# Block-product chunks of a feed-forward layer: the place of two down slabs and of one product, and the homes of the raw blocks

## The chip, the cores and the metric

The kernel runs on one core of a Trainium2 chip. The metric is the device time of one launch in microseconds, as the median of several runs. One more run is recorded by the hardware profiler, and all durations of single instructions come from that execution. The engines are TensorE (PE in the profile, with PEld for its weight loads), VectorE (DVE), ScalarE (ACT), GpSimd (POOL) and SyncE (SP), which here only issues DMA transfers. Each engine works through a queue of its own in order; semaphores tie the queues together.

## The reference

The kernel computes two layers of a model on 256 tokens of width 1024, all in float32. A layer has four stages, each closed by a layer norm over the residual sum. Two of the four are feed-forward stages (FFN), and only those are touched here:

```python
def swiglu(x, w_gate, w_up, w_down):
    return (jax.nn.silu(x @ w_gate) * (x @ w_up)) @ w_down

for l in range(DEPTH):
    h = layer_norm(ALPHA * h + 0.5 * swiglu(h, ffn1_gate[l], ffn1_up[l], ffn1_down[l]), ...)
    ...   # mixer, cross attention
    h = layer_norm(ALPHA * h + 0.5 * swiglu(h, ffn2_gate[l], ffn2_up[l], ffn2_down[l]), ...)
```

`w_gate` and `w_up` are 1024 x 2816, `w_down` is 2816 x 1024.

## The kernel before, in words

**Precision.** TensorE multiplies in a reduced float32 form, so each float32 operand is split in two parts (`split`, L60-62): ScalarE casts the high part (`whi`, L61) and VectorE subtracts it from the source to get the low part (`wlo`, L62). A product is then three matmuls: high by high, low by high, high by low (`product`, L109-112). Each weight tile that arrives by DMA (128 x 1024 float32, 512 KB, called `raw`) costs one cast and one subtraction. High and low parts go round over eight buffers each; raw tiles with the tag `raw` go round over six.

**An FFN.** `ffn` (L407) cuts the 2816 inner columns in six chunks, five of 512 and one of 256, and writes the work of a chunk after the other (main loop, L727-755). Chunk 0 is made by `first`, chunk 5 by `last_hidden`, and the others by `hidden` or, where the chunk's number is in `sevens` (L694), by `by_seven` (L575-667). `sevens` is (2, 3, 4), except for the first FFN of layer 0, where it is (3, 4): eleven chunks in all. When the activations of a chunk exist, `turn` (L451-464) deals them out with four DMA issues on SP (L455), transposes them on VectorE (L458) and splits them. They are then multiplied with the rows of `w_down`: `slab(c, u)` (L688) loads half `u` of chunk `c`'s rows (two raw tiles, so two casts and two subtractions) and `both(c, u)` (L711-717) issues its 24 matmuls for all four output quarters (eight products of three). These add over all chunks into four banks of PSUM with the tag `dn`; the chunks' own products use four banks with the tag `acc`.

**A chunk of block products.** Gate and up chunk are each cut in two by rows: `w00` (gate, rows 0-3 of eight row tiles), `w10` (gate, rows 4-7), `w01` (up, 0-3), `w11` (up, 4-7). Each block is two raw tiles. With tokens in two halves as well, a plain evaluation takes eight products of 12 matmuls; `by_seven` takes seven, with sums of blocks on the weights' side (additions on VectorE, L606, in place in the raw tiles) and sums of quarters of x on the other side (`bx`, made once for an FFN). The products, in the order of the code before:

1. `w00` into bank `o[0]`
2. `w00 + w01` into `o[1]`
3. `w00 + w01 + w11`, added to what is in `o[0]`
4. `w10` into `o[2]`
5. `w01 + w11`, added to `o[0]`
6. `w11`, added to `o[1]`
7. `w00` with gate's rows 4-7 added to it (after the third product the raw tile is reduced and refilled so by an accumulating DMA that GpSimd issues, L644), added to `o[0]`

Since several products add to one bank, what the bank holds in between has to be copied out before the next may add to it: `taken` (L634-635) is a ScalarE copy of `o[0]`, done after products 1, 3 and 5. `put` (L624-625) is a VectorE addition or subtraction of a bank and a stored half. `left` closes the chunk (activation, last subtraction, the product gate by up at L664, and `turn`).

**Homes.** The raw tiles of the blocks live in borrowed places: a pair `spare0`, `spare1`, a pair `lng`, `lnb` (free until the layer norm's parameters are loaded into them by `ln_params`, L300-305, after the last block chunk), and tiles of the tag `raw`. In the kernel before, `w00` and `w01` exchange the first two pairs from chunk to chunk, `w11` is always in two `raw` tiles, and `w10` in `spare2` and a `raw` tile (L595-600).

**The order of the work.** The order in which the code issues instructions is not quite the order in which they run: a scheduler, when the kernel is built, sorts the instructions of each engine into one fixed queue by the dependencies and its own estimates. At run time each queue is served in order. A DMA issue stands in the queue of SP (or GpSimd) and waits there until its target is free.

The three FFNs with three block chunks have the same order on all engines, in either kernel.

Of the kernel before, what the change touches and what calls it, by code (L numbers as in the profile page):

```python
# [11 lines left out]
AF = mybir.ActivationFunctionType  # L12
ALU = mybir.AluOpType
# [4 lines left out]
P = 128  # L18
# [10 lines left out]
CHUNK = 512  # L29
# [17 lines left out]
def model(ctx: ExitStack, tc: tile.TileContext, t: dict, out: bass.AP):  # L47
    nc = tc.nc
# [5 lines left out]
    def acc(shape=(P, 2, SEQ), tag="acc"):  # L54
        return ps.tile(list(shape), F32, tag=tag, name=tag)
# [4 lines left out]
    def split(hi, lo, src):  # L60
        nc.scalar.copy(hi, src)  # L61
        lows.append(nc.vector.tensor_tensor(lo, src, hi.bitcast(F32), op=ALU.subtract))  # L62
# [73 lines left out]
    def mm_rows(o, xh, xl, wh, wl, start, stop, more=False):  # L136
        product(o, xh, wh, start, False, more)
        product(o, xh, wl, False, False, more)
        product(o, xl, wh, False, stop, more)

    def tok(i):
        return slice(i * P, (i + 1) * P)
# [264 lines left out]
    def ffn(l, name, n, pend=None, last=False, early=None):  # L407
        gate, up, down = (t[f"{name}_{x}"][l] for x in ("gate", "up", "down"))
        with tc.tile_pool(name="ffn", bufs=2, reuse_waits="tile") as fp:
# [24 lines left out]
            def ordered(v):  # L434
                return v.rearrange("p (a k j) -> p a k j", a=4, j=32)

            def in_order(o):
                return o.rearrange("p (a j k) -> p a k j", a=4, j=32)
# [136 lines left out]
            def by_seven(c0, bx, between):  # L575
                def rows_by_columns(r):
                    return r.rearrange("p (k c) -> p k c", c=CHUNK)

                def pieces(*tags):
                    return [  # L580
                        rows_by_columns(
                            (fp if "spare" in g else wp).tile([P, DM], F32, tag=g, name="raw", bufs=6 if g == "raw" else 1)
                        )
                        for g in tags
                    ]

                def block(m, j, to):
                    for i in range(2):
                        k = 4 * j + 2 * i
                        loads.append(nc.sync.dma_start(  # L590
                            to[i], m[k * P : (k + 2) * P, c0 : c0 + CHUNK].rearrange("(k p) c -> p k c", p=P)
                        ))
                    return to

                homes = [("spare0", "spare1"), ("lng", "lnb")]  # L595
                turn_of = sevens.index(c0 // CHUNK) % 2
                w00 = block(gate, 0, pieces(*homes[turn_of]))
                w01 = block(up, 0, pieces(*homes[1 - turn_of]))
                w11 = block(up, 1, pieces("raw", "raw"))
                w10 = block(gate, 1, pieces("spare2", "raw"))  # L600

                def parts_of(r, plus=None):
                    hi, lo = [], []
                    for i in range(2):
                        if plus is not None:
                            nc.vector.tensor_tensor(r[i], r[i], plus[i], op=ALU.add)  # L606
                        h = wp.tile([P, 1024], F32R, tag="whi", name="whi", bufs=8)
                        w = wp.tile([P, 1024], F32R, tag="wlo", name="wlo", bufs=8)
                        h, w = (rows_by_columns(x) for x in (h, w))
                        split(h, w, r[i])  # L610
                        hi.append(h)
                        lo.append(w)
                    return Weights(hi, lo, 2, [])

                def part_of_x(i, j):
                    d = slice(4 * j, 4 * j + 4)
                    return xTh[:, d, tok(i)], xTl[:, d, tok(i)]

                def run(o, x, w, more=False):
                    for k in range(4):  # L620
                        wh, wl = w.at(k, slice(0, CHUNK))
                        mm_rows(o, x[0][:, k, :], x[1][:, k, :], wh, wl, k == 0 and not more, k == 3, more)

                def put(o, a, op, b):  # L624
                    nc.vector.tensor_tensor(ordered(o), in_order(a), ordered(b), op=op)

                s = activations()  # L630
                ef = fp.tile([P, NT, CHUNK], F32, tag="up", name="halves", bufs=1)
                e, f = ef[:, 0, :], ef[:, 1, :]

                def taken(o, bank):  # L634
                    nc.scalar.copy(ordered(o), in_order(bank))  # L635

                o = [acc((P, CHUNK)) for _ in range(2)]
                run(o[0], part_of_x(0, 0), parts_of(w00))
                taken(s[:, 0, :], o[0])
                run(o[1], bx[0], parts_of(w00, w01))  # L640
                run(o[0], bx[1], parts_of(w00, w11), True)
                for i in range(2):
                    k = 4 + 2 * i
                    nc.gpsimd.dma_start(  # L644
                        w00[i], gate[k * P : (k + 2) * P, c0 : c0 + CHUNK].rearrange("(k p) c -> p k c", p=P),
                        accum_op=ALU.add,
                    )
                taken(e, o[0])
                o.append(acc((P, CHUNK)))
                run(o[2], part_of_x(0, 1), parts_of(w10))  # L650
                run(o[0], bx[2], parts_of(w01, w11), True)
                put(s[:, 0, :], o[2], ALU.add, s[:, 0, :])
                nc.scalar.activation(s[:, 0, :], s[:, 0, :], AF.Silu)
                taken(f, o[0])
                between()
                put(f, o[1], ALU.subtract, f)
                run(o[1], bx[3], parts_of(w11), True)
                run(o[0], part_of_x(1, 1), parts_of(w00), True)


                def left():
                    activate(s, 1, o[0])
                    put(e, o[1], ALU.subtract, e)
                    nc.vector.tensor_tensor(s, s, ef, op=ALU.mult)  # L664
                    return turn(s)

                return left
# [20 lines left out]
            def slab(c, u):  # L688
                w = load(down, c * 4 + 2 * u, 2, 0, DM, dealt=c < len(chunks) - 1)
                ah, al = acts[c]  # L690
                return w, ah[:, 2 * u : 2 * u + 2, :], al[:, 2 * u : 2 * u + 2, :]


            sevens = (2, 3, 4) if early is None else (3, 4)  # L694
            bx = []
# [7 lines left out]
            chunks = [(c, min(CHUNK, DFF - c)) for c in range(0, DFF, CHUNK)]  # L703
# [7 lines left out]
            def both(c, u):  # L711
                a = slab(c, u)
                for i in range(NT):
                    for k in range(2):
                        for m in range(2):
                            apart = last and i == m == k == u == 1 and c == 3
                            rows_of(a, i, k, m, c == u == k == 0, apart)
# [9 lines left out]
            for c, (c0, ncol) in enumerate(chunks):  # L727
                if not c:
                    acts.append(first())
                    ys = [[acc((P, 512), "dn") for _ in range(2)] for _ in range(NT)]  # L730
                elif c in sevens:
                    left = by_seven(c0, bx, lambda: both(c - 2, 1))
                else:
                    if c in (1, 2) and early is not None:
                        acts.append(hidden(c0, aside))
                    else:
                        acts.append(hidden(c0) if ncol == CHUNK else last_hidden(c0))
                if c == 1 and early is None:
                    bx.extend(blocks_of_x())
                if c == max(sevens) + 1:  # L740
                    gb = ln_params(l, n)
                if c == 1 and early is not None:

                    with tc.issue_after(loads[-1].ins):
                        rest = early(fp)
                if c == 2 and early is not None:
                    with tc.issue_after(lows[-1].ins):
                        rest[0]()
                if c > 0:
                    if c > 1 and c not in sevens:  # L750
                        both(c - 2, 1)
                    if c < len(chunks) - 1:
                        both(c - 1, 0)
                    if c in sevens:
                        acts.append(left())
            end = [slab(4, 0), slab(4, 1), slab(5, 0)]

            def tail(i, m, cols, alone, between):
# [477 lines left out]
```

## Time and profile before

| | |
|---|---|
| median of three runs | 1084.16 us (1083.94 to 1084.78) |
| the profiled execution | 1086.89 us |
| its span (first to last instruction) | 1085.2 us |
| granted TensorE clock, mean | 0.997 |
| TensorE busy | 1059.0 us |
| VectorE busy | 969.0 us |
| ScalarE busy | 669.1 us |
| GpSimd busy | 91.5 us |
| read from device memory | 227.69 MB |

The profile's page gives these totals. The trace behind it can be asked for stretches of time (busy time of each engine, granted clock, DMA share and rate), for an engine's timeline (start and duration of each instruction or group of like ones, and in brackets how long the engine idled before it and what ended the wait), for landing times of DMA transfers, and for the chain of work that ended last. In the rows, L61 and the like are lines of the kernel before; `out<-in` are the program's names. The durations of consecutive instructions on VectorE and ScalarE overlap a little, since the tail of one runs beside the start of the next. Matmuls are pipelined in the same way.

The four stretches with block chunks lie at 76 to 151, 421 to 513, 592 to 685 and 955 to 1047 us.

### The profile page before, as it was taken

What the parts mean: (1) busy time and instruction counts of PE and PEld (TensorE: products, weight loads), DVE (VectorE), ACT (ScalarE), POOL (GpSimd) and SP (SyncE); (2) the same over time, 40 slices, a digit from 0 to 9 for tenths busy, and PEclk for the clock granted to TensorE, in tenths of its full rate; (3) what the DMA queues carried; (4) which work ended last, traced back from release to release, by engine and by line L of the source; (5) the groups of instructions that cost most, each with busy time, mean ns of one, the idle gap of its engine ahead of it and who ended that gap; (6) DMA issues with size and microseconds to landing.
All of it is one profiled execution on the core that took longest, in us unless ns stands there. A gap on an engine that the chain in (4) does not pass through costs nothing.

```text
span 1085.2 us, 16259 instructions
## 1 busy us (share of the span) xinstructions
PE 1059.0 (98%) x5918; PEld 927.8 (85%) x5918; DVE 969.0 (89%) x1279; ACT 669.1 (62%) x920; POOL 91.5 (8%) x136
## 2 busy tenths in 40 slices
PE   9998999999999999999999999999999999999997
PEld 7887788989899888888888887888898998888786
DVE  6979987998998799999899999888989788999996
ACT  7547675767457566567575677666764655667661
POOL 9600001000000000000000000010000000000000
PEclk9999999999999999999999999999999999999999
DMA  9997595755575587679776787957536664786691
GB/s 361 266 290 209 160 322 181 254 195 166 165 271 176 177 278 201 209 259 268 237 276 191 270 271 190 300 181 241 182 131 210 240 238 166 252 271 192 196 291 40
DMA packets 136882, 243.45 MB, mean 224 GB/s; under 512 B 9761, under 2 KB 48961, under 8 KB 136801
## 3 DMA queue, kind: packets, MB, share of 16 engines
q1 hardware_dynamic: 129024, 228.49, 62.4%
q0 software_dynamic: 7200, 12.73, 7.0%
q10 hardware_dynamic: 576, 1.18, 0.3%
q8 instruction: 46, 0.75, 0.3%
q14 instruction: 36, 0.29, 0.1%
HBM read 227.69 MB, written 1.05 MB: 211 GB/s over the span
## 4 chain that ended last, share of the span: by engine, by line
PE 69%; DVE 15%; DMA 7%; issue 5%; ACT 3%; SPq 0%; DVEq 0%; ACTq 0%
PE acc L112 45%; PE dn L112 21%; DVE wlo L62 8%; DMA raw<-in_ffn_up_dram 3%; DMA raw<-in_ffn_gate_dram 3%; DVE raw L606 3%; ACT whi L61 2%; DMA dealt<-sg 1%; PE acc L179 1%; DVE square L458 1%; DVE sg L664 1%; PE dn L938 1%; DVE al L62 1%; DVE sg L445 0%; SPq L455 0%
## 5 line engine op out<-in xcount | busy, mean ns | idle before, releaser
L61 ACT CAST whi<-raw 128x1024 fp32r<-128x1024 f32 (+1 forms) x462 | 463.7, 1041 | 184.4 <-DVE raw L606 79.0
L62 DVE TENSOR_TENSOR wlo<-raw,whi 128x1024 fp32r<-128x1024 f32 (+1 forms) x462 | 542.5, 1207 | 27.2 <-ACT whi L61 24.4
L112 PE MATMUL acc<-whi,xT 128*128 128x512 f32 x872 | 268.5, 381 | 5.0 <-ACT whi L61 4.8
L112 PEld LDWEIGHTS acc<-whi,xT 128*128 128x128 f32 x872 | 164.9, 189 | 30.5 <-ACT whi L61 7.4
L112 PE MATMUL acc<-wlo,xT 128*128 128x512 f32 x436 | 165.8, 380 | 3.5 <-DVE wlo L62 3.5
L112 PE MATMUL acc<-xT,whi 128*128 128x512 f32 x576 | 142.2, 382 | 0.2
L112 PE MATMUL dn<-whi,ah 128*128 128x512 f32 x346 | 130.1, 381 | 1.4 <-ACT whi L61 1.4
L112 PE MATMUL dn<-wlo,ah 128*128 128x512 f32 x346 | 131.4, 380 | 0.0
L112 PE MATMUL dn<-whi,al 128*128 128x512 f32 x346 | 131.1, 379 | 0.0
L112 PEld LDWEIGHTS acc<-xT,whi 128*128 128x128 f32 x576 | 104.0, 190 | 12.5 <-ACT whi L61 0.7
L112 PEld LDWEIGHTS acc<-wlo,xT 128*128 128x128 f32 x436 | 82.4, 189 | 16.8 <-DVE wlo L62 5.4
L112 PE MATMUL dn<-whi,xT 128*128 128x512 f32 x288 | 87.8, 381 | 0.0
L606 DVE TENSOR_TENSOR raw<-raw 128x1024 f32<-128x1024 f32 x66 | 78.7, 1215 | 1.7 <-DMA raw<-in_ffn_up_dram 1.6
L112 PEld LDWEIGHTS acc<-xT,wlo 128*128 128x128 f32 x576 | 75.5, 191 | 3.9
L112 PE MATMUL acc<-xT,wlo 128*128 128x256 f32 x576 | 75.9, 275 | 0.0
L112 PEld LDWEIGHTS dn<-whi,ah 128*128 128x128 f32 x346 | 65.1, 189 | 12.0 <-ACT whi L61 3.0
L112 PE MATMUL acc<-whi,kTh 128*128 128x512 f32 x176 | 68.5, 389 | 5.8 <-ACT sg L635 3.8
L112 PEld LDWEIGHTS dn<-wlo,ah 128*128 128x128 f32 x346 | 65.4, 189 | 10.0 <-DVE wlo L62 0.9
L112 PEld LDWEIGHTS dn<-whi,al 128*128 128x128 f32 x346 | 65.4, 189 | 9.2
L112 PE MATMUL acc<-wlo,kTh 128*128 128x512 f32 x176 | 67.7, 385 | 0.8 <-DVE wlo L62 0.8
L112 PE MATMUL acc<-whi,kTl 128*128 128x512 f32 x176 | 67.5, 383 | 0.0
L112 PEld LDWEIGHTS dn<-whi,xT 128*128 128x128 f32 x288 | 54.4, 189 | 7.7 <-DVE xT L62 0.3
(235 smaller groups left out, 1297.0 us busy)
## 6 DMA issues: line engine op xcount, KB each, us to landing
raw<-in_ffn_up_dram SPq DMA_DIRECT2D x88, 512.0 KB, 5.8
raw<-in_ffn_down_dram SPq DMA_DIRECT2D x88, 512.0 KB, 5.7
raw<-in_ffn_gate_dram SPq DMA_DIRECT2D x84, 512.0 KB, 5.3
raw<-in_w_in_dram SPq DMA_DIRECT2D x48, 512.0 KB, 4.7
raw<-in_ffn_gate_dram POOLq DMA_DIRECT2D x22, 512.0 KB, 6.4
dealt<-sg SPq DMA_DIRECT2D x80, 128.0 KB, 3.2
raw<-in_ca_k_dram SPq DMA_DIRECT2D x16, 512.0 KB, 4.9
raw<-in_w_out_dram SPq DMA_DIRECT2D x16, 512.0 KB, 4.4
```

What stands on the lines that cost most here:

```text
L61: nc.scalar.copy(hi, src)
L62: lows.append(nc.vector.tensor_tensor(lo, src, hi.bitcast(F32), op=ALU.subtract))
L112: nc.tensor.matmul(o, w, x, start=start, stop=stop, skip_group_check=more)
L179: nc.tensor.transpose(pt[:, k, :], src[:, (4 * j + k) * P : (4 * j + k + 1) * P], unit)
L458: nc.vector.transpose(d[:, i].rearrange("p k (b r) -> p b k r", b=4), x[:, :, i, :].rearrange("p b (k j) -> p b k j", k=4),)
L606: nc.vector.tensor_tensor(r[i], r[i], plus[i], op=ALU.add)
L664: nc.vector.tensor_tensor(s, s, ef, op=ALU.mult)
L938: nc.tensor.matmul(o[g, hh, :], kc[:, hh, g], x, start=True, stop=True)
```

## The change

The diff touches `by_seven` and the main loop:

- Three homes instead of two: block chunk number `n` of an FFN puts `w00`, `w01` and `w11` into the homes `n`, `n + 1` and `n + 2` modulo 3, where the third home is two `raw` tiles. `w10` stays in `spare2` and a `raw` tile, and its loads are issued before those of `w11`.
- The product with `w10` (number 4 above) is issued as the third, and its bank is allocated at the start with the two others.
- Half 1 of the down slab of the chunk two before (`both(c - 2, 1)`) is issued ahead of the fifth product instead of between the fifth and the sixth.
- Half 0 of the down slab of the chunk before (`both(c - 1, 0)`), which followed the seventh product, is issued between the fifth product and the sixth.
- `left`, which closes the chunk, follows the seventh product directly.

```diff
-                homes = [("spare0", "spare1"), ("lng", "lnb")]
-                turn_of = sevens.index(c0 // CHUNK) % 2
-                w00 = block(gate, 0, pieces(*homes[turn_of]))
-                w01 = block(up, 0, pieces(*homes[1 - turn_of]))
-                w11 = block(up, 1, pieces("raw", "raw"))
+                homes = [("spare0", "spare1"), ("lng", "lnb"), ("raw", "raw")]
+                n = sevens.index(c0 // CHUNK)
+                w00 = block(gate, 0, pieces(*homes[n % 3]))
+                w01 = block(up, 0, pieces(*homes[(n + 1) % 3]))
                 w10 = block(gate, 1, pieces("spare2", "raw"))
+                w11 = block(up, 1, pieces(*homes[(n + 2) % 3]))
...
-                o = [acc((P, CHUNK)) for _ in range(2)]
+                o = [acc((P, CHUNK)) for _ in range(3)]
                 run(o[0], part_of_x(0, 0), parts_of(w00))
                 taken(s[:, 0, :], o[0])
                 run(o[1], bx[0], parts_of(w00, w01))
+                run(o[2], part_of_x(0, 1), parts_of(w10))
                 run(o[0], bx[1], parts_of(w00, w11), True)
...
+                put(s[:, 0, :], o[2], ALU.add, s[:, 0, :])
                 taken(e, o[0])
-                o.append(acc((P, CHUNK)))
-                run(o[2], part_of_x(0, 1), parts_of(w10))
+                between[0]()
+                nc.scalar.activation(s[:, 0, :], s[:, 0, :], AF.Silu)
                 run(o[0], bx[2], parts_of(w01, w11), True)
-                put(s[:, 0, :], o[2], ALU.add, s[:, 0, :])
-                nc.scalar.activation(s[:, 0, :], s[:, 0, :], AF.Silu)
                 taken(f, o[0])
-                between()
+                between[1]()
                 put(f, o[1], ALU.subtract, f)
                 run(o[1], bx[3], parts_of(w11), True)
                 run(o[0], part_of_x(1, 1), parts_of(w00), True)
...
-                    left = by_seven(c0, bx, lambda: both(c - 2, 1))
+                    left = by_seven(c0, bx, [lambda: both(c - 2, 1), lambda: both(c - 1, 0)])
...
                 if c > 0:
-                    if c > 1 and c not in sevens:
-                        both(c - 2, 1)
-                    if c < len(chunks) - 1:
-                        both(c - 1, 0)
                     if c in sevens:
                         acts.append(left())
+                    else:
+                        if c > 1:
+                            both(c - 2, 1)
+                        if c < len(chunks) - 1:
+                            both(c - 1, 0)
```

## The prediction

> **What bounds the kernel now.** I read the totals by engine first, then busy time by stretch, then VectorE's timeline through one block-product stretch, and last TensorE's gaps and the chain of waits there.
>
> ```profile
> span 1085.2 us, 16259 instructions
> ...
> PE 1059.0 (98%) x5918; PEld 927.8 (85%) x5918; DVE 969.0 (89%) x1279; ACT 669.1 (62%) x920; POOL 91.5 (8%) x136
> ```
>
> TensorE is busy 98% of the span, so at most 26 us are to be had anywhere without removing matmuls, and the change removes none. The stretches tell where those 26 us lie (columns: stretch, length, busy PE, PE load, VectorE, ScalarE, GpSimd, granted clock, DMA share, GB/s):
>
> ```profile
> 76.00:151.00 75.00, 69.61 (x313) 59.71 (x312) 74.68 (x86) 50.26 (x58) 4.85 (x4) 0.98 0.71 214
> 421.00:513.00 92.00, 88.55 (x400) 74.68 (x400) 88.84 (x86) 64.35 (x73) 6.00 (x6) 1.00 0.82 248
> 592.00:685.00 93.00, 88.84 (x402) 74.92 (x401) 89.66 (x86) 64.63 (x74) 5.99 (x5) 1.00 0.82 246
> 955.00:1047.00 92.00, 88.51 (x401) 74.61 (x400) 90.25 (x87) 64.29 (x74) 5.96 (x5) 1.00 0.81 248
> 150.00:405.00 255.00, 254.90 (x1685) 228.09 (x1684) 218.60 (x354) 156.77 (x254) 8.93 (x13) 1.00 0.64 210
> 690.00:955.00 265.00, 264.91 (x1724) 236.61 (x1723) 230.15 (x365) 160.32 (x257) 10.00 (x14) 1.00 0.62 208
> ```
>
> The first four rows are the four FFNs' block-product stretches (two chunks in the first, three in the others); TensorE idles 5.39, 3.45, 4.16 and 3.49 us in them, and 0.1 us in the two long rows between. So the change can only take from 16.5 us. In the same four rows VectorE is busy 74.68 of 75.00, 88.84 of 92, 89.66 of 93 and 90.25 of 92. A block chunk asks of VectorE 18 subtractions for weights, 6 additions of blocks, three 512-wide operations, one product and a pair of transposes with a subtraction behind. The durations are these (VectorE's timeline, second FFN of layer 0):
>
> ```profile
> 408.07 1.18 DVE L606 TENSOR_TENSOR raw<-raw 128x1024 f32<-128x1024 f32 x1
> ...
> 417.72 0.68 DVE L445 TENSOR_TENSOR sg<-acc,sg 128x512 f32<-128x512 f32 x1
> ...
> 419.45 1.22 DVE L606 TENSOR_TENSOR raw<-raw 128x1024 f32<-128x1024 f32 x1
> 421.85 5.77 DVE L62 TENSOR_TENSOR wlo<-raw,whi 128x1024 fp32r<-128x1024 f32 x5 [1.19 <-ACT whi L61]
> 427.54 1.30 DVE L458 STREAM_TRANSPOSE square<-dealt 128x512 f32<-128x512 f32 x2
> ...
> 440.72 1.23 DVE L62 TENSOR_TENSOR wlo<-raw,whi 128x1024 fp32r<-128x1024 f32 x1 [0.50 <-ACT whi L61]
> 442.22 1.23 DVE L606 TENSOR_TENSOR raw<-raw 128x1024 f32<-128x1024 f32 x1 [0.28 <-DMA raw<-in_ffn_up_dram]
> ...
> 468.05 6.89 DVE L62 TENSOR_TENSOR wlo<-raw,whi 128x1024 fp32r<-128x1024 f32 x6
> ...
> 483.41 3.49 DVE L606 TENSOR_TENSOR raw<-raw 128x1024 f32<-128x1024 f32 x3
> 486.81 1.22 DVE L62 TENSOR_TENSOR wlo<-raw,whi 128x1024 fp32r<-128x1024 f32 x1
> ```
>
> Six subtractions in 6.89 us overlap by one tail: (6.89 - 1.22) / 5 = 1.134 us each. A 512-wide operation occupies about 0.60, a pair of transposes 1.22. A chunk is 26 of 1024 width (29.5), three of 512 (1.8) and the transposes (1.2): 32.5 us. TensorE's rate comes from the chain of waits:
>
> ```profile
> 502.40 5.18 PE acc L112 x24
> 507.58 5.18 PE dn L112 x24
> 512.76 2.29 PE acc L112 x14
> ```
>
> 24 matmuls in 5.18 us are 0.216 us each; a chunk has seven products of 12 and two slabs of 24, 132 matmuls, 28.5 us. VectorE sets the pace inside the block chunks by some 4 us a chunk, and TensorE's queue, full when the stretch begins, runs dry towards its end.
>
> **The change part by part.** Removed: nothing. Matmuls, casts, subtractions, additions and bytes are those of before. Moved: the product with gate rows 4 to 7 (`w10`) comes before the third product; the first slab moves up to before the fifth product; the second slab moves from behind the seventh product to before the sixth; the closing operations follow the seventh at once; the loads of `w10` come before those of `w11`; and homes turn over three places.
>
> *VectorE.* Between 408.07 and the end of the last addition (486.81) of the third block chunk, VectorE works through 71 rows: 61 of 1.134, eight of 0.60, two pairs of transposes of 1.22, 76.5 us. 486.81 - 408.07 = 78.7, so it idled 2.2 there (1.19 + 0.50 + 0.28 are quoted). I followed the changed queue, in which the same 71 rows stand, row by row at these durations. The 1.19 goes: in the changed order another addition stands between the addition at 419.45 and the subtraction that needs its cast. In its place come: transposes 0.25 late, since the activations are dealt out by four issues on SP, which take 2.6 us in all, and the last lands 6.2 us after its issue (the 420.42 row below); two subtractions in all 0.9 behind slabs' buffers, because two slabs now sit ahead of the last two products; one addition 0.55 behind a load into a home that the chunk before has only just left; 0.3 in small ones. That is 2.0 against 2.2: -0.2 of VectorE's time.
>
> The load is the term that I am least sure of. Its home is free when VectorE has taken the last low part of the previous chunk from it, near 438.2 by my walk, and the addition wants it at 443.6. Loads on that queue land as follows (the busiest stretch, and the page's medians):
>
> ```profile
> 436.24 1.50 SPq L590 DMA_DIRECT2D raw<-in_ffn_up_dram  x2
> ...
> 420.42 6.16 DMA dealt<-sg
> ...
> 436.24 5.89 DMA raw<-in_ffn_up_dram
> ...
> raw<-in_ffn_up_dram SPq DMA_DIRECT2D x88, 512.0 KB, 5.8
> ...
> raw<-in_ffn_gate_dram SPq DMA_DIRECT2D x84, 512.0 KB, 5.3
> raw<-in_ffn_gate_dram POOLq DMA_DIRECT2D x22, 512.0 KB, 6.4
> raw<-in_w_in_dram SPq DMA_DIRECT2D x48, 512.0 KB, 4.7
> ```
>
> I take 5.9, the row measured at this very place, so 444.1; the ends are 4.7 (no wait, the light stages) and 7.6 (the median of four gate loads issued from 424 to 438 us, when DMA is at its ceiling):
>
> ```profile
> raw<-in_ffn_gate_dram SPq DMA_DIRECT2D x4, 512.0 KB, 7.6
> ```
>
> *TensorE's end.* TensorE's last dry spot before the stretch ends is at the start of the third chunk's additions:
>
> ```profile
> 487.89 0.48 PE L112 MATMUL acc<-whi,xT 128*128 128x512 f32 x1 [1.41 <-ACT whi L61]
> ...
> 490.40 0.48 PE L112 MATMUL acc<-wlo,kTh 128*128 128x512 f32 x1 [0.25 <-DVE wlo L62]
> ...
> 484.71 3.13 ACT L61 CAST whi<-raw 128x1024 fp32r<-128x1024 f32 x3 [3.50 <-DVE raw L606]
> 487.74 0.58 ACT L635 COPY sg<-acc 128x512 f32<-128x512 f32 x1
> ```
>
> From 490.40 on TensorE is gapless up to the next chunk at 512.6 (507.58 + 5.18, less the tail by which a modelled end overlaps the next start). In the changed order, TensorE waits instead at the third product, because that product adds to the bank of the first, and ScalarE must first have copied the bank out. In ScalarE's changed queue the copy stands behind the casts of the two slab pieces and of one sum block. VectorE's last addition ends at 486.6; then one cast to 487.75 (3.13 / 3 = 1.04, 0.95 in a run), two slabs and a sum at 0.95 each, the waits between, and the copy from 491.55 to 492.1. TensorE then has 92 matmuls left: 92 x 0.216 = 19.9, hence 512.0, and 0.5 for small waits as at 490.40: 512.5 against 512.6 now. Without that copy in the way it would be 510.9. Sum for this FFN: -0.1.
>
> *Layer 1.* Both of its FFNs carry the same three orders on all engines as the FFN just walked, before and after. The last one has the same gaps, so -0.1. The first one has, besides, two load waits:
>
> ```profile
> 613.28 1.23 DVE L606 TENSOR_TENSOR raw<-raw 128x1024 f32<-128x1024 f32 x1 [0.42 <-DMA raw<-in_ffn_up_dram]
> ...
> 648.24 1.22 DVE L606 TENSOR_TENSOR raw<-raw 128x1024 f32<-128x1024 f32 x1 [0.52 <-DMA raw<-in_ffn_up_dram]
> ```
>
> 0.94 against 0.28 in the FFN walked; the changed order has one such wait of 0.55, so it is worth 0.4 more: -0.5.
>
> *First FFN of layer 0*, two block chunks. TensorE waits before its third product, and the next matmuls are slow:
>
> ```profile
> 94.49 0.48 PE L112 MATMUL acc<-whi,kTh 128*128 128x512 f32 x1 [3.35 <-ACT sg L635]
> ...
> 98.40 0.63 PE L112 MATMUL acc<-whi,kTl 128*128 128x512 f32 x1
> ...
> 91.00:94.50 3.50, 0.14 (x2) 0.01 (x1) 3.50 (x4) 3.50 (x6) 1.20 (x1) 1.00 0.94 150
> 94.50:98.50 4.00, 4.00 (x12) 3.26 (x13) 4.00 (x11) 3.98 (x4) 0.00 (x0) 0.62 0.98 199
> ```
>
> 3.35 us idle, then some 3.4 us at a granted clock of 0.62, matmuls 0.43 apart instead of 0.216: about 1.5 lost. The `w10` product now fills this place: up to 4.8 for TensorE. But VectorE is busy 74.68 of 75.00 in this stretch and its work is unchanged, so the time turns up later: in the second chunk TensorE comes to the first slab at 123.6 and finds its high part cast only at 127.1 and its low part at 129.7, because a product, three additions and two subtractions stand ahead on VectorE. I arrive at an end of 149.5 at full clock, and with half the loss of a slow spell after that 3.4 us wait 150.5, against 150.8 before: -0.3.
>
> [...]
>
> *Covers.* The moved loads of `w10` cost nothing while VectorE is late for them; without that cover each place that a load falls back in the SP queue is 0.75 (two issues took 1.50). The second slab was what TensorE did while VectorE closed the chunk (445 to 458: copy, product, four deals, transposes); that work must now lie under the next chunk's first products, which by my walk leaves 1.3 us to spare at the last chunk instead of some 6.
>
> Sum: -0.1 - 0.5 - 0.1 - 0.3 = -1.0 on the profiled execution, 1086.89 (span 1085.2 and 1.7 around it), hence 1085.9. That execution is 2.7 above the median 1084.16, which I take as the base: **1083.2 us**. A difference below 0.2% (2.2 us) counts as no change for this kernel.
>
> **The rivals.**
> *Faster: the copy isn't late.* If ScalarE reaches the copy as soon as the product is done, three FFNs end 1.6 sooner (4.8), and if VectorE's new waits stay out, 0.5 in each as well (1.5); with the 0.5 and the 0.3 above, -7.1: 1077. For it: ScalarE has idle time in every row of the stretches (64 of 92). Against it: its queue is in order, and its casts follow VectorE's additions.
> *Slower: loads into the third home land late.* The home is freed by the last low part of the chunk before, and five loads are then issued within 5 us. At 5.9 VectorE waits 0.55; at 7.6 it waits 2.2, and the third chunk's load, whose slack is 0.3 by the walk, adds 1.4. Nothing behind makes it up, as VectorE sets the pace: 3 x (1.7 + 1.4) = +9.3 at worst, and about half of it where only one load an FFN comes in the busy part: +5.5, 1089. The bound of 0.2% is reached at 6.8 us of landing time (0.9 on the one load and 0.6 on the other, less the 0.4 that the forecast is worth, in each of the three). For it:
>
> ```profile
> 430.00:436.00 6.00, 5.48 (x26) 4.47 (x25) 6.00 (x6) 5.29 (x7) 0.00 (x0) 1.00 1.05 401
> ```
>
> DMA share 1.05 at 401 GB/s just there. Against it: the 5.89 quoted was measured inside this busy time.
> *Clock.* If the wait in the first FFN's second chunk costs a full slow spell, that FFN ends at 151.1 and the total is 0.6 higher: 1083.8. It doesn't change the sign.
> *The change doesn't do what it says.* A scheduler orders the queues, so this could be; but in the built kernel the orders are as described above, save that the first slab's matmuls partly precede the third product. I give it nothing of its own.
>
> **How the numbers follow.** Forecast (VectorE keeps the pace, gaps move) 0.36, clock 0.08, faster rival 0.29, slower rival 0.27. The likeliest one's own range is 1080 to 1087, by the small waits (0.5 in each of four FFNs either way, and one load landing at 4.7 or 7). Of the forecast's 0.36, 0.06 lies below 1082 and 0.06 above 1086.3; with the clock's 0.08 in the middle: faster 0.35, same 0.32, slower 0.33. The range over all cases is 1077 to 1090.
>
> **What would show it.** After: the gap before the third product of the first FFN (94.49) is gone, with the 0.62 clock there; a gap of about 3 us stands in its second chunk before a slab. In the other FFNs TensorE's gaps still sum to 3 to 4 us a stretch, the largest (some 4 us) before the third product of the third chunk, released by the copy. VectorE's busy time is 969 within 1, and its share in the four stretches stays above 96%. Landing times of `w11` near 6 us confirm the load term; above 6.8 with VectorE waiting on loads in each FFN, the slower rival holds. I am wrong if the stretches shrink by more than 2 us each, or if a gap appears at the last chunk, where I expect the 1.3 us to suffice.

## The result, and the profile after

The changed kernel takes 1102.11 us (median of four runs, 1100.49 to 1103.49) against 1084.47 for the kernel before (median of four, one more than was known at the prediction): the ratio is 1.0155, with a 95% interval of 1.0136 to 1.0173. It is 17.6 us slower, where 1 us less was predicted. The profiled execution took 1103.49 us, of which the span is 1101.7.

The totals of the page, kernel after:

```profile
span 1101.7 us, 16338 instructions
...
PE 1068.7 (97%) x5918; PEld 933.9 (85%) x5918; DVE 971.1 (88%) x1279; ACT 671.6 (61%) x920; POOL 93.0 (8%) x136
...
PE 81%; DVE 7%; DMA 5%; issue 3%; ACT 2%; SPq 1%; DVEq 0%; ACTq 0%
```

TensorE has the same 5918 matmuls but is 9.7 us longer busy, and it idles 6.8 us more; VectorE is 2 us longer busy and idles 14 us more. The place can be told exactly, because outside the FFNs both kernels run in step (104.8 us in either from the transposes at 192.15, before 190.59, to those at 296.99, before 295.42): TensorE's transposes that follow each FFN (L179) come 1.6 us later than before after the first FFN, 6.9 after the second, 10.5 after the third, and the span is 16.5 longer. The four FFNs cost +1.6, +5.3, +3.6 and +6.0 us. The second is taken here, since it was walked in the prediction. VectorE's timeline of the kernel after:

```profile
409.64 1.18 DVE L62 TENSOR_TENSOR wlo<-raw,whi 128x1024 fp32r<-128x1024 f32 x1
...
438.35 3.82 DVE L62 TENSOR_TENSOR wlo<-raw,whi 128x1024 fp32r<-128x1024 f32 x3 [0.60 <-ACT whi L61]
...
446.68 2.36 DVE L606 TENSOR_TENSOR raw<-raw 128x1024 f32<-128x1024 f32 x2 [1.65 <-DMA raw<-in_ffn_up_dram]
...
479.43 3.71 DVE L606 TENSOR_TENSOR raw<-raw 128x1024 f32<-128x1024 f32 x3 [1.11 <-DMA raw<-in_ffn_up_dram]
...
487.07 2.35 DVE L62 TENSOR_TENSOR wlo<-raw,whi 128x1024 fp32r<-128x1024 f32 x2
489.34 3.49 DVE L606 TENSOR_TENSOR raw<-raw 128x1024 f32<-128x1024 f32 x3
492.74 3.49 DVE L62 TENSOR_TENSOR wlo<-raw,whi 128x1024 fp32r<-128x1024 f32 x3
```

From the transposes' end (409.64, where the kernel before has 408.07) to the end of the last addition, VectorE now takes 492.74 - 409.64 = 83.1 us instead of 78.7. The two subtractions at 487.07, ahead of the last additions, are those of `w10`; before, they came behind. The two waits on up loads are 2.76 together, before 0.28. TensorE, in its timeline and in busy time by stretch (columns as in the prediction):

```profile
493.82 1.13 PE L112 MATMUL dn<-whi,ah 128*128 128x512 f32 x4 [2.68 <-ACT whi L61]
496.19 0.80 PE L112 MATMUL acc<-whi,kTh 128*128 128x512 f32 x1 [1.24 <-ACT sg L635]
```

```profile
490.90:493.80 2.90, 0.24 (x2) 0.00 (x0) 2.90 (x3) 2.81 (x4) 0.00 (x0) 1.00 0.70 189
493.80:496.20 2.40, 1.14 (x5) 0.68 (x5) 2.40 (x4) 2.40 (x4) 1.94 (x2) 0.83 0.03 3
496.20:501.50 5.30, 5.30 (x13) 4.21 (x14) 5.30 (x8) 5.20 (x6) 0.48 (x1) 0.50 1.01 188
```

The dry spot that was 1.41 and 0.25 us before is one of 2.68 and 1.24 with four matmuls between, and behind it the granted clock is 0.50 for 5.3 us, in which TensorE gets through 13 matmuls. The chain of waits shows the same piece, and what came before it:

```profile
472.12 7.23 DMA raw<-in_ffn_up_dram
...
485.93 1.23 DVE sg L664
...
489.17 3.15 DMA dealt<-sg
...
493.67 1.99 ACT whi L61 x2
495.66 0.49 ACT sg L635
...
496.19 5.49 PE acc L112 x12
501.68 4.63 PE dn L112 x20
```

Twelve matmuls take 5.49 us here and 2.59 at full clock: 2.9 lost, 3.1 with those that follow. Between the load and the casts, the chain runs over VectorE's next additions and subtractions, the product that closes the second chunk (485.93) and the deals of its result. The last deal landed at 492.3; the copy into `sg` stands behind five casts in ScalarE's queue and ran at 495.6.

### The profile page after: what moved, and what is told of

Same layout as the page of the kernel before. It is cut to its first block, busy times and chain, and to the rows that moved or that the text cites. A ratio compares the mean times of both kernels' runs of the same rounds, so it can differ in the third digit from the quotient of the medians.

```text
span 1101.7 us, 16338 instructions
## 1 busy us (share of the span) xinstructions
PE 1068.7 (97%) x5918; PEld 933.9 (85%) x5918; DVE 971.1 (88%) x1279; ACT 671.6 (61%) x920; POOL 93.0 (8%) x136
## 4 chain that ended last, share of the span: by engine, by line
PE 81%; DVE 7%; DMA 5%; issue 3%; ACT 2%; SPq 1%; DVEq 0%; ACTq 0%
PE acc L112 54%; PE dn L112 25%; DVE wlo L62 3%; DMA raw<-in_ffn_up_dram 3%; DMA dealt<-sg 2%; ACT whi L61 1%; DVE raw L606 1%; PE acc L179 1%; SPq L455 1%; DVE sg L664 1%; PE dn L939 1%; DVE square L458 0%; DVE halves L625 0%; ACT ah L61 0%; PE dn L998 0%
## 5 line engine op out<-in xcount | busy, mean ns | idle before, releaser
L112 PE MATMUL dn<-wlo,ah 128*128 128x512 f32 x346 | 134.1, 388 | 3.5 <-DVE wlo L62 3.5
L112 PE MATMUL dn<-whi,al 128*128 128x512 f32 x346 | 133.5, 388 | 0.8 <-DVE al L62 0.3
```

Source lines behind the costliest of these rows:

```text
L112: nc.tensor.matmul(o, w, x, start=start, stop=stop, skip_group_check=more)
```

## The experiments

My theory at this point was A: the new order makes TensorE's idle time come in one piece, and the half clock behind it (0.50 for 5.3 us) is the cost. The rivals were B, the rotating homes' late loads from which the rest follows; C, VectorE's pace alone, with the clock only filling what would be idle; and, formed on the way, D (the second slab as a cover) and E (the copy into `sg` late).

Three parts were put on the kernel before one by one and in pairs, so that all eight combinations are known. H stands for the homes together with the order of the loads (the two were not taken apart), W for the `w10` product as the third, S for the slabs.

**H alone.**

```diff
+                homes = [("spare0", "spare1"), ("lng", "lnb"), ("raw", "raw")]
+                n = sevens.index(c0 // CHUNK)
...      # w00, w01, w10, w11 as in the change; the rest as before
```

> The kernel before with one part of the change: the three homes that go round, and the loads of w10 ahead of those of w11. Slabs and products stay where they were. Theory A (the new order makes TensorE's idle time come in one piece, long enough for the clock to fall; the homes matter little): within 2 us of before, VectorE's waits on loads grow by no more than 1 us an FFN. Theory B (loads into the rotating homes land late, and everything else follows from that): slower by 5 to 9 us, with 1.5 to 3 us of VectorE's waits on the up loads in each of the three FFNs with three block chunks.

**W and S without H** (the changed kernel with the six lines on homes of before).

> The changed kernel with the two homes and the load order of before; slabs and the w10 product stay where the change put them. Theory A: still 9 to 14 us slower than before, with a stretch of half clock in each FFN. Theory B: about 1085 to 1087, no waits on up loads beyond 0.5 us an FFN and no half clock in the three FFNs with three block chunks.

**W alone.**

```diff
+                run(o[2], part_of_x(0, 1), parts_of(w10))
                 run(o[0], bx[1], parts_of(w00, w11), True)
...
-                run(o[2], part_of_x(0, 1), parts_of(w10))
```

> The kernel before with the w10 product as the third and nothing else. Theory A: the gap of 3.35 us and the half clock in the first FFN (94.5 us) go, and the other FFNs change by less than 1 us each, since the slabs still lie where TensorE needs them: 1080 to 1084. Theory B: the same. A cost of more than 2 us here would speak against both, for this part alone.

**S alone.**

```diff
+                between[0]()
                 run(o[0], bx[2], parts_of(w01, w11), True)
...
-                between()
+                between[1]()
...      # the main loop as in the change
```

> The kernel before with the two slabs moved in between the products and the closing operations right behind the seventh, nothing else. Theory A: the slabs are what filled TensorE's time while VectorE closed a chunk; without them its idle time comes in one piece and the clock falls: 5 to 14 us slower. Theory B: within 3 us of before.

**H and S, H and W.**

> Homes and slabs as in the changed kernel, the w10 product still fourth. If the parts add up, the moved slabs cost 28 us and the homes give back about 12 (what they give between the run with old homes and the changed kernel): 1098 to 1103, and the w10 product's move is then worth nothing beside the others. If moving the w10 product costs here what it costs alone (13 us), this one is at 1087 to 1090.

> Homes and the w10 product as in the changed kernel, the slabs as before. Alone, the w10 product's move cost 13 us, of which 2.8 in each of three FFNs are waits on the up loads. If the rotating homes take those waits away: 1090 to 1093. If they don't: 1097 to 1100.

What the eight gave (ratio to the kernel before on the same chip, and VectorE's time in wait for up loads ahead of its additions, from the groups of instructions):

| parts | median us | ratio, 95% interval | waits on up loads, us |
|---|---|---|---|
| none (before) | 1084.47 | 1 | 1.6 |
| H | 1083.26 | 0.9980 [0.9967, 0.9992] | 0 |
| W | 1099.18 | 1.0119 [1.0104, 1.0135] | 7.9 |
| S | 1113.61 | 1.0253 [1.0230, 1.0276] | 8.9 |
| H, W | 1093.80 | 1.0078 [1.0063, 1.0093] | 0 |
| H, S | 1103.73 | 1.0164 [1.0146, 1.0181] | 0.9 |
| W, S | 1114.14 | 1.0260 [1.0244, 1.0275] | 14.7 |
| H, W, S (changed) | 1102.11 | 1.0155 [1.0136, 1.0173] | 8.3 |

Rows of that view for three of them, in turn W, H with W, and W with S:

```profile
L606 DVE TENSOR_TENSOR raw<-raw 128x1024 f32<-128x1024 f32 x66 | 78.7, 1218 | 8.0 <-DMA raw<-in_ffn_up_dram 7.9
```

```profile
L606 DVE TENSOR_TENSOR raw<-raw 128x1024 f32<-128x1024 f32 x66 | 78.7, 1223 | 0.2
```

```profile
L606 DVE TENSOR_TENSOR raw<-raw 128x1024 f32<-128x1024 f32 x66 | 78.6, 1219 | 15.1 <-DMA raw<-in_ffn_up_dram 14.7
```

Of these expectations only that for H came close, on theory A's side (2.3 us faster, where 2 either way were allowed). W alone was to change little (1080 to 1084) and cost 13 us, which by the words of its expectation speaks against A and B alike. S alone, and W with S, cost 28 us, twice what A allowed. H with S and H with W came out less than 1 us above their ranges.

What follows. The rotating homes, with their order of loads, are the one part that helps. They take 1.6 us of waits on loads away from the kernel before and 6.4 to 8 us in the other three pairs, and bring 2 to 11 us; alone they are faster than before. My theory B (the rotating homes bring late loads) falls; the late loads of the changed kernel come from the order of products and slabs, and would be worse with the old homes. The slabs carry the loss: 20 us on top of H. The `w10` product costs 13 us alone, and with the slabs moved nothing (H, S against all three).

For W the reason can be seen. In H with W, TensorE waits before the fifth product:

```profile
464.51 0.48 PE L112 MATMUL acc<-whi,kTh 128*128 128x512 f32 x1 [2.13 <-ACT halves L635]
```

In the whole execution, such waits for copies into `halves` sum to 9.2 us; with H alone the same row has none:

```profile
L112 PE MATMUL acc<-whi,kTh 128*128 128x512 f32 x176 | 70.3, 400 | 12.2 <-ACT halves L635 9.2 <-ACT whi L61 2.2 <-ACT sg L635 0.8
```

```profile
L112 PE MATMUL acc<-whi,kTh 128*128 128x512 f32 x176 | 68.3, 388 | 3.3 <-ACT sg L635 3.3
```

The fifth product adds to the bank of the third, and ScalarE has to copy that bank out in between. In the kernel before, the `w10` product lay between them and covered the copy. With W alone, nothing does; in the changed kernel the first slab takes that place.

**Which slab.** With H, once the first slab alone was moved and once the second.

```diff
+                between()
                 run(o[0], bx[2], parts_of(w01, w11), True)
...
-                between()
                 put(f, o[1], ALU.subtract, f)
```

```diff
                 taken(f, o[0])
-                between()
+                between[0]()
+                between[1]()
                 put(f, o[1], ALU.subtract, f)
...      # the main loop as in the change
```

> Rotating homes, and of the two slabs only the first moved: half 1 of the chunk two before goes ahead of the fifth product, half 0 of the chunk before stays behind the seventh. With both moved the kernel was some 20 us slower than with the homes alone. Theory D (a slab is cheap on VectorE, 2.3 us for 5.2 us of TensorE, and the one behind the seventh product is the cover under which VectorE prepares the next chunk's first products): little changes here, 1083 to 1087. If the first slab's place is what costs: 1095 to 1103.

> Rotating homes, and the second slab alone moved: both slabs stand between the fifth and the sixth product, the closing operations follow the seventh at once. Theory D: most of the 20 us, 1097 to 1105, with the matmuls left after the last dry spot of an FFN's block chunks more numerous, or that spot later. If the first slab's place is what costs: 1083 to 1088.

The first gave 1090.80 us, ratio 1.0048 [1.0033, 1.0063], the second 1113.64, ratio 1.0257 [1.0239, 1.0275]. So the slab behind the seventh product is the one not to be moved: it costs 30 us against H, and having the first ahead of the fifth product gives 10 of these back. Both expectations of theory D were missed: the first (1083 to 1087) by 4 us, the second (1097 to 1105) by 9, so the place of the first slab matters too, and that of the second more than D had it. ScalarE's timeline in the run with the second slab moved:

```profile
465.26 1.04 ACT L61 CAST whi<-raw 128x1024 fp32r<-128x1024 f32 x1
470.60 0.59 ACT L635 COPY sg<-acc 128x512 f32<-128x512 f32 x1 [4.30 <-DMA dealt<-sg]
```

The copy of the first product's bank writes into `sg`, which has one buffer, and the chunk before is still being dealt out of it. In the kernel before, a slab ran on TensorE meanwhile. In all, ScalarE waits 15.5 us for the deals in this run:

```profile
L635 ACT COPY sg<-acc 128x512 f32<-128x512 f32 x11 | 6.4, 583 | 15.7 <-DMA dealt<-sg 15.5
```

**Is it the buffer?** `sg` got two buffers. Their memory was taken from the low parts, which go round over seven buffers instead of eight, and one run has that alone.

```diff
-                return fp.tile([P, NT, CHUNK], F32, tag="sg", name="sg", bufs=1)
+                return fp.tile([P, NT, CHUNK], F32, tag="sg", name="sg", bufs=2)
...
-                w = wp.tile([P, 1024], F32R, tag="wlo", name="wlo", bufs=8)
+                w = wp.tile([P, 1024], F32R, tag="wlo", name="wlo", bufs=7)
```

> The control: the changed kernel with seven buffers for low parts, nothing else. Both theories: 1100 to 1108, within some us of the changed kernel.

> The changed kernel with two buffers for the activations (sg) instead of one; their 4 KB a partition are taken from the low parts, which go round over seven buffers instead of eight. Theory E (the copy of the first product's bank comes late since its target is still being dealt out): the copy runs soon after the first product, the dry spot before the third product goes, 5 to 12 us faster than the control with seven low buffers. Theory C (VectorE's pace alone): within 3 us of the control.

> Rotating homes and the second slab moved (1113.6 us), with two buffers for the activations and seven for low parts. Theory E: ScalarE's waits of 4.3 and 5.4 us on the deals go, with TensorE's 1.5 to 2.6 us ahead of the third product: 1098 to 1106. Theory C: 1110 or more.

> Rotating homes alone (1083.3 us) with two buffers for the activations and seven for low parts. Here the slab behind the seventh product covers the deals, and the copy was not late: within 2 us of the run with the homes alone by either theory, unless seven low buffers cost something by themselves.

The changed kernel took 1118.39 us with seven low buffers and 1109.56 with the second `sg` besides: 8.8 less, inside what theory E allows. The control itself was to be within some us of the changed kernel and is 16 above it. ScalarE's timelines in the second FFN show what the second buffer does, first with seven low buffers alone, then with two `sg`:

```profile
497.92 5.02 ACT L61 CAST whi<-raw 128x1024 fp32r<-128x1024 f32 x5 [5.20 <-DVE raw L606]
502.85 0.57 ACT L635 COPY sg<-acc 128x512 f32<-128x512 f32 x1
```

```profile
492.49 0.58 ACT L635 COPY sg<-acc 128x512 f32<-128x512 f32 x1
497.81 5.97 ACT L61 CAST whi<-raw 128x1024 fp32r<-128x1024 f32 x6 [4.74 <-DVE raw L606]
```

With the second buffer the copy stands ahead of the casts in ScalarE's queue, and not behind them. So in the changed order the one buffer acts through the queue as it is built and not by a wait at run time: in all three runs of this order, with one `sg` or two, ScalarE's copies into `sg` wait 0.0 us for the deals. Part of the 8.8 is the clock (0.994 in the mean over the profiled execution against 0.986).

But with the second slab moved, the second `sg` took the wait on the deals away (15.5 to 0) and the time rose from 1113.6 to 1127.5; and with the homes alone it rose from 1083.3 to 1095.7. The last two have no control of their own. If the missing low buffer costs them about what it costs the changed kernel (16 us), the second `sg` bought them some 2 to 4 us; without that control this is not shown. It fits that, with the second slab moved, TensorE's waits that end with ScalarE's copies fall only from 15.5 to 11.4 us with the second `sg`, while those that end with VectorE's subtractions rise from 12.1 to 18.1 (to which the missing low buffer may add). So the wait on the deals, where it is plain to see, is at most a part of what sets the time.

**The half clock.** Matmuls whose result is not used were put into the dry spot of each FFN's last block chunk, twelve at first, then 26, meant to fill the whole of it.

```diff
+                    with tc.issue_after(last_of_w10.ins):
+                        for k in range(12):
+                            nc.tensor.matmul(o[3], xTh[:, 4, tok(0)], xTh[:, 4:6, :], start=True, stop=True)
```

> The changed kernel with twelve added matmuls (2.6 us of TensorE) into an unused bank in each FFN's last block chunk, between the w10 product and the first slab, where TensorE idled 2.7 to 3.1 us. Their result is not used. Theory A (half clock after the merged idle time is a cost of its own): the half clock in these four places goes and the kernel with more work is 7 to 10 us faster than the changed one, about 1093. Theory C (VectorE sets the time, the clock only fills what would be idle): 1100 to 1103, unchanged.

> The changed kernel with 26 added matmuls (5.6 us) in each FFN's last block chunk, in the whole of the place where TensorE idles there, between the w10 product and the third one. In the run with twelve the half clock still came in some executions. Theory A: no half clock in that place in any execution, and 4 to 8 us faster than the changed kernel, 1094 to 1098. Theory C (VectorE alone sets the time): 1100 to 1104.

Twelve: 1101.33 us, ratio 1.0154 [1.0133, 1.0174]; 26: 1105.36, ratio 1.0174 [1.0149, 1.0200]. Neither is faster than the changed kernel, so theory A, which promised 7 to 10 us from the first and 4 to 8 from the second, falls as I had stated it. In the profiled execution with twelve, the clock stays up (1.00) in the place shown above (the row is that stretch, 2.0 us later since the first FFN is):

```profile
496.00:499.00 3.00, 1.33 (x5) 0.78 (x5) 3.00 (x4) 3.00 (x5) 2.42 (x2) 1.00 0.20 20
499.00:503.00 4.00, 4.00 (x20) 3.50 (x19) 4.00 (x6) 4.00 (x6) 0.00 (x0) 1.00 0.96 203
```

There the second FFN is 1.6 us shorter than in the changed kernel, the third 1.7, the last 3.1 (163.3, 162.4 and 173.0 us between the transposes against 165.0, 164.1 and 176.1), but the first 2.0 longer. Over the four executions of that kernel the mean clock was 0.997 once (1099.17 us) and 0.989 to 0.991 three times (1100.25 to 1104.60); the trace is of the first of these, so where the clock fell in the other three is not shown. With 26 the clock was 0.994 to 0.997 throughout and the time no better. That run tests less than it seems: the third product now precedes the first part of the slab, so it has more behind it, and in three FFNs the added matmuls outlast the copy. The copy ends at 499.97, 675.08 and 1041.65 us, and the third product starts behind the added matmuls at 500.54, 677.22 and 1042.97, which is 0.6 to 2.1 us later.

So a spell costs its FFN up to 3 us where it comes (by the 1.6, 1.7 and 3.1 above), and the order of the work costs the rest with or without it. How the 17 us divide exactly between the two was not settled, but single executions narrow it. With H and S, one at a mean clock of 0.996 took 1102.96 us and one at 0.987 took 1105.31; with the twelve added matmuls, the one at 0.997 took 1099.17. W alone was 13 us slower than before at clocks of 0.993 to 0.997. By these few executions I estimate the clock at some 3 us of the 17; most of the loss comes without it.

**Less for VectorE.** With H, the two additions that make `w01 + w11` in each chunk were moved to GpSimd.

```diff
-                            nc.vector.tensor_tensor(r[i], r[i], plus[i], op=ALU.add)
+                            (on or nc.vector).tensor_tensor(r[i], r[i], plus[i], op=ALU.add)
...
-                run(o[0], bx[2], parts_of(w01, w11), True)
+                run(o[0], bx[2], parts_of(w01, w11, nc.gpsimd), True)
```

> Rotating homes with slabs and products as before, and the two additions of w01 and w11 of each block chunk moved from VectorE to GpSimd. If VectorE's pace is what leaves TensorE dry, 2.3 us less a chunk on VectorE take most of what is left of the dry spots: 1074 to 1080. If GpSimd is too slow for the place or slows VectorE beside it: 1084 to 1095.

It took 1129.37 us, ratio 1.0401 [1.0385, 1.0417], far above both ranges of its expectation. Groups of instructions, GpSimd's additions and VectorE's:

```profile
L606 POOL TENSOR_TENSOR raw<-raw 128x1024 f32<-128x1024 f32 x22 | 84.4, 3840 | 280.2 <-DVE raw L606 165.5 <-DMA raw<-in_ffn_up_dram 55.4 <-DMA raw<-in_ffn_down_dram 38.8
...
L606 DVE TENSOR_TENSOR raw<-raw 128x1024 f32<-128x1024 f32 x44 | 61.4, 1413 | 0.2
```

An addition takes GpSimd 3.8 us in the mean, three times what VectorE needs, and VectorE's own additions grow from 1.22 to 1.41 us in the mean. With this price on both engines, the run can't say what a VectorE with less to do would bring.

**The best of both.** H, and W in the first FFN alone.

```diff
+                if early is not None:
+                    o.append(acc((P, CHUNK)))
+                    run(o[2], part_of_x(0, 1), parts_of(w10))
                 run(o[0], bx[1], parts_of(w00, w11), True)
```

> The rotating homes, and the w10 product third in the first FFN alone, where its move was worth 1.7 us (the 3.3 us of idle time and the half clock at 94 us); everything else as before. Sum of the two measured parts: 1081 to 1082, faster than before and than the changed kernel. If the gain of the first FFN is given back behind it: 1083.

1084.32 us, ratio 0.9986 [0.9978, 0.9995]: faster than before, not than H alone. The first FFN's idle 3.3 us at 94 us goes, but a wait of 2.7 us on a low part of the slab takes its place at 99.8:

```profile
99.79 0.48 PE L112 MATMUL dn<-wlo,ah 128*128 128x512 f32 x1 [2.69 <-DVE wlo L62]
```

The gain is given back, as the second half of the expectation had it. Both this run and H alone (0.9980) beat both kernels, by 0.1 to 0.2%; their intervals overlap, and H alone is the simpler.

## Why the prediction was wrong

What held. VectorE's and TensorE's work are nearly unchanged (VectorE's 971.1 us against 969.0 is a little over the 1 us allowed; 5918 matmuls). The idle time at 94.49 us in the first FFN and the slow clock behind it are gone (1.00 from 94 to 98 us), and a wait before the slab of its second chunk takes their place, 1.3 us earlier than forecast and 3.08 us long (3.5 forecast). In the second and the last FFN the largest dry spot lies where it was put, before the third product of the third chunk; its first part ends with a cast for four matmuls of the slab, its second with the copy. With 2.68 and 1.24, and 2.84 and 0.94, it has the length forecast. In the third FFN it is shorter (1.27 and 1.25). The last chunk's activations were in time. The sum of TensorE's gaps did not hold: 4.3, 6.3, 5.0 and 6.8 us in the four stretches, not 3 to 4. Besides the forecast gaps, one stands in the second chunk of each longer FFN, before the first slab (1.60 and 0.75, 1.73 and 0.75, 1.73 and 0.75), where the kernel before idled 0.96.

What failed, by the steps of the prediction, for the second FFN (-0.1 forecast, +5.3 measured):

- *"in which the same 71 rows stand".* A miscount. The changed queue has 73 rows up to the last addition, since the two low parts of `w10` now come ahead of it (487.07). 2 x 1.134 = +2.3 us.
- *"I take 5.9, the row measured at this very place, so 444.1".* This was the shortest of what the trace of before shows there: of its four up loads issued between 429 and 438 us, the pair quoted took 5.9 and 6.1, the other pair 7.0 and 7.2. In the changed kernel the first loads waited for were issued at 439.6 and 472.1 and landed 7.0 and 7.2 us later. I had named 6.8 as the point from which the slower rival decides. VectorE's idle time is 83.1 - 78.7 = 4.4 (73 rows are 78.7) against 2.0 in the sum: +2.4, of which the waits on loads are 2.2 (2.76 against 0.55).
- *"two slabs and a sum at 0.95 each, the waits between, and the copy from 491.55".* With VectorE later, nothing was left to wait for: the five casts ran in one piece, and the copy ended 3.3 us after the last addition, not 5.5: -2.2.
- *"Clock."* This rival was priced for the first FFN alone, at 0.6 us. I had forecast one dry spot of some 4 us in three more FFNs, at which the same price had to be set (in the kernel before, 3.35 us of idle time are followed by a clock of 0.62), and did not set it. Here: +3.1.
- *"0.5 for small waits".* None were left: -0.5.

-0.1 + 2.3 + 2.4 - 2.2 + 3.1 - 0.5 = 5.0, of 5.3 measured. This is an account of the execution profiled; that taking the clock's 3.1 away would bring as much is not shown (with twelve added matmuls this FFN got 1.6 shorter). By the same rows the third and the last FFN had the miscount and the late loads too (1.77 in the third FFN, 1.77 and 1.97 in the last), and each a spell of half clock at its last dry spot (0.52 from 672.7 to 676.1, 0.51 from 1039.8 to 1045 us); the third had a second spell behind the gap in its second chunk (granted clock 0.64 from 640 to 643 us). The first FFN, forecast at -0.3, came to +1.6. Its wait of 3.08 was followed by a second one of 1.22 and by twelve slow matmuls, 5.4 us instead of 2.6 (granted clock 0.50 from 128.3 to 133.6): the whole loss and not half of it, and nearly twice the 1.5 read from the kernel before.

The slower rival had the right sign and its condition was met, but its cause was misnamed: *"loads into the third home land late"*. By the code, both late loads above go into `spare0`, `spare1` and not into the third home, and the runs show that the rotation with its load order relieves the loads (8.9 to 0.9 us of waits with the slabs moved, 14.7 to 8.3 with both). By the order of the queues, with the slabs inside the chunk VectorE frees the homes of the last two products later and the slabs' own loads go ahead of theirs; that this is the reason was not tried by itself.

The deeper fault is in *"Covers"*. I asked only whether the work of the second slab was needed at the last chunk (1.3 us to spare). What it covered was the start of each following chunk: a slab is 5.2 us of TensorE for two subtractions (2.3 us) of VectorE, a sum block's product 2.6 us of TensorE for 4.5 of VectorE (at the 0.216 us a matmul and 1.134 a row of the prediction). With the slab gone from between the chunks, three and more products that VectorE can't keep up with stand in a row. That the second slab alone costs 30 us against the homes alone shows where it lay; that VectorE's pace is the reason was argued from the rows, and is supported, though not shown, by the run in which the wait on the deals was taken away and the time did not fall. The place of the copy in ScalarE's queue, which goes with the one `sg` buffer, has a part in it, as the 8.8 us of the second buffer suggest.

How long an idle time has to be for the clock to fall is not shown by the trace of after. It fell after 2.68 and 1.24 us with 0.9 us of matmuls between (0.50), and also after 1.27 and 1.25 (0.52). After 1.73 and 0.75 us it fell in the third FFN (0.64 from 640 to 643 us) and stayed up in the last (1.00 from 1004.9 to 1008).

## What to carry to other kernels

Before work is moved, write down for each piece how much of the pacing engine's time it asks for and how much of the other engine's time it gives; a piece that gives more than it asks is a cover, and what it covers is whatever runs behind it, in every round of the loop and not at the end alone. When idle times are moved into one place, price the clock for every such place (here the slow matmuls of the second FFN lost 3.1 us). Count the rows of the two queues by a list and not by hand: two rows too few on the engine that sets the pace (2.3 us in one FFN) were more than the whole effect that was forecast (1.0). Take a load's time from all loads of the busy stretch (here 5.9 to 7.2 us), not from one pair.

## What was not expected of the hardware

A buffer of low parts fewer (seven instead of eight) costs the changed kernel 16 us (1118.39 against 1102.11), in part outside the FFNs (the stretch between the transposes at 192 and 297 us grew by 0.6 us): this is as much as the whole change lost. That the cause is how far VectorE may run ahead was not tried by itself. The granted clock is not the same from one execution to the next: of one and the same kernel, the one with twelve added matmuls, the mean clock was 0.997 in one execution and 0.989 to 0.991 in three, with 1 to 5 us between them.
